# Pairing the two heads of a 128-partition block: score and value products of neighbourhood attention taken head beside head, the state product of linear attention in one operand

## The chip, the cores and the metric

The kernel runs on one core of a Trainium2 chip. The metric is the device time of one execution in microseconds (us); lower is better. A time is given as the median of several runs. A profiled execution gives the rows shown below: TensorE (PE, with its weight loads as PEld), VectorE (DVE), ScalarE (ACT), GpSimd (POOL), and the DMA queues.

## The reference, cut to what matters

Two layers are run over 640 tokens: 128 context tokens and 512 latent tokens, model width 1024. Each layer normalises its input, projects it, and feeds three groups in parallel; their outputs go through one output projection and are added to the input. An expert lookup (PEER) follows. Only two of the groups are touched here.

- **Linear attention**, 6 heads of 64, in both directions. For each chunk of tokens a 64x64 state per head and direction is read by the decayed queries:

```
inter = jnp.einsum('bhtk,bhkv->bhtv', qc * jnp.exp(cum), s)
...
return s_new, inter + intra
```

- **Neighbourhood attention**, 6 heads of 64. The latent tokens form a grid of 8 rows by 64 columns; a query sees the columns near its own (all 8 rows) and all 128 context keys, in one softmax. Context queries see the context keys only.

```
s_win = jnp.einsum('bhrqd,bhrkd->bhrqk', qg, kw).astype(jnp.float32) * scale + bias
s_win = jnp.where(col_mask[None, None, None], s_win, -1e30)
s_ctx = jnp.einsum('bhrqd,bhcd->bhrqc', qg, k_ctx).astype(jnp.float32) * scale
p = jax.nn.softmax(jnp.concatenate([s_win, s_ctx], axis=-1), axis=-1).astype(v.dtype)
```

## The kernel before, in words

Activations lie feature-major: features on the 128 partitions, tokens along the free axis. 128 partitions hold a pair of heads, head 0 of the pair on partitions 0 to 63 and head 1 on 64 to 127. There are three pairs (`fc` = 0, 1, 2) in each group and each layer (`l` = 0, 1), so a piece of work that is done once for a pair is done six times in all. Everything here is f32. An f32 matmul appears in the trace as two PE instructions (two passes), each with its own weight load; a transpose and an fp32r matmul appear as one.

`mix(l)` computes, in the order of the program, linear attention for three pairs (`pre`, line 286: the projections and decays; `gla`, line 316), one half of the convolution (`conv`, line 436), then neighbourhood attention for three pairs (`napre`, line 459: three projections and the transposed values; `na`, line 479), the other half of the convolution and the output projection. A projection (`projw`, line 218) is 48 fp32r matmuls at line 227 into two PSUM banks; its weights are split into a high and a low part by ACT (line 211) and DVE (line 212).

The order in which the instructions stand on an engine is fixed when the program is built and is not that of the text. A scheduler goes through the ready instructions in program order and puts later ones into the gaps. So in the trace the projections of pair `fc + 1` stand between the attention steps of pair `fc`, and in the last pair those of the convolution and of the output projection do. Buffers of one tag are handed out in program order: the PSUM tag "s" has four banks, and `ps_s` (scores), `pt` (transposes) and, in layer 0, the adaLN rows `ps_ada` and `ps_at` (lines 147 and 157) take turns in them.

**Neighbourhood attention** (`na`). For each head `hh` of the pair and each of five query tiles `qt` (one of context, four of latent tokens), one step is: scores against 1, 2 or 3 key tiles (line 493 or 500) and against the context keys (line 502), both with a contraction over the 64 partitions of that head; on DVE the bias is added and the maximum taken in one instruction (line 505); the maximum is negated (509); ACT takes the exponential with its sum (510); DVE inverts the sum and scales (511, 512); PE transposes the 1, 3 or 4 tiles of probabilities (516); ACT copies them out of PSUM (518); and PE multiplies them with the values (521), 64 output partitions wide, into the half of the bank `npo` that belongs to the head. Per head the five tiles have 1, 3, 4, 4 and 3 key tiles, 15 in all. Head 0 goes through all five tiles before head 1. In layer 0 a piece of the adaLN matmuls (`ada_steps`, line 152) is drawn after each tile of head 1. Those put four blocks of 32 output partitions into one bank.

**Linear attention** (`gla`). `qz[d]` holds the decayed queries of direction `d` twice: slot 0 has head 0 on partitions 0 to 63 and zeros below, slot 1 zeros and then head 1. Both slots are needed at line 355, where the two heads have to stay apart. The zeros are written once per layer (line 283). The states `sts[d]` are block-diagonal, with zeros off the diagonal (line 284). Line 413 multiplies each slot with the state: four matmuls for each of four latent chunks, two heads by two directions, all into one accumulation. Line 323 writes `qz` anew for the next pair. Line 333 multiplies keys and queries of each head, contraction over 64 partitions, into one bank for each head.

Of the kernel before, what the change touches and what calls it, by code (L numbers as in the profile page):

```python
# [10 lines left out]
F32 = mybir.dt.float32  # L11
# [12 lines left out]
TP, TS = 128, 512  # L24
# [9 lines left out]
NAK = [(0, 2), (0, 3), (1, 3), (2, 2)]  # L34
BOFF = {0: (0, 384), 1: (384, 512), 2: (384, 512), 3: (896, 384)}
BW = 1280
C_BADA, C_N1, C_N2, C_BAF, C_BAB, C_CW, C_CB, C_GN, C_FN = 0, 48, 56, 64, 67, 70, 76, 78, 81
NVEC = 89
CH_LR, CH_Q, CH_K, CH_V, CH_G, CH_CH, CH_CB, CH_CC, CH_QN, CH_KN, CH_VN = 0, 1, 4, 7, 10, 13, 15, 17, 19, 22, 25
# [26 lines left out]
class Trunk:  # L66
# [164 lines left out]
    def mix(self, l):  # L231
        tc, nc, I, O = self.tc, self.nc, self.I, self.O
        V, S, G, PE = self.V, self.S, self.G, self.PE
# [82 lines left out]
        def gla(fc, X):  # L316
# [20 lines left out]
            for lb in range(7):  # L337
# [38 lines left out]
                    nt.append(t2)  # L376
                tot = nt
            for d in range(2):
                kt = gp.tile([128, 5, 128], F32, name="kt", tag="kt")
                tokmajor(kS[d], kt)  # L380
                pk = pss.tile([128, 128], F32, name="pk", tag="s")
                PE.matmul(pk, kt[:, 0, :], vt[:, 0, :], start=True, stop=True)
                so = gp.tile([128, 64], F32, name="so", tag="so", bufs=2)
                for hh in range(2):
                    r = slice(64 * hh, 64 * hh + 64)
                    S.activation(so[r, :], pk[r, r], AF.Copy)
                nc.sync.dma_start(O["st"][l, d, fc], so)
                s = sts[d]
                order = range(4) if d == 0 else range(3, -1, -1)
                prev = None  # L390
                pk = pss.tile([128, 4, 128], F32, name="pk", tag="s")
                for c in order:
                    if prev is None:
                        for hh in range(2):
                            r = slice(64 * hh, 64 * hh + 64)
                            nc.sync.dma_start(s[r, c, r], I["st0"][l, d, fc, r, :])
                    else:
                        PE.matmul(pk[:, prev, :], kt[:, prev + 1, :], vt[:, prev + 1, :], start=True, stop=True)
                        for hh in range(2):
                            r = slice(64 * hh, 64 * hh + 64)  # L400
                            V.scalar_tensor_tensor(s[r, c, r], s[r, prev, r], tot[d][r, prev + 1:prev + 2],
                                                   pk[r, prev, r], op0=OP.mult, op1=OP.add)
                    prev = c
            for g, (c0, c1) in enumerate(CG):
                n = c1 - c0
                po = pss.tile([128, 4, 128], F32, name="po", tag="s")
                for c in range(n):
                    cs = slice((c + c0) * 128, (c + c0 + 1) * 128)
                    first = True
                    if g:  # L410
                        for d in range(2):
                            for hh in range(2):
                                PE.matmul(po[:, c, :], qz[d][:, hh, cs], sts[d][:, c, :], start=first, stop=False)
                                first = False
                    for hh in range(2):
                        r = slice(64 * hh, 64 * hh + 64)
                        PE.matmul(po[:, c, r], att[:, c0 + c, hh, :], vt[:, c0 + c, r], start=not g,
                                  stop=bool(hh) or not g)
                pv = po[:, :n, :].rearrange("p c (h v) -> p (c h) v", h=2)
                sq = gp.tile([128, 8, 64], F32, name="osq", tag="osq")  # L420
                S.activation(sq[:, :2 * n, :], pv, AF.Square)
                ms = gp.tile([128, 8], F32, name="oms", tag="oms", bufs=2)
                V.tensor_reduce(ms[:, :2 * n], sq[:, :2 * n, :], axis=AX.X, op=OP.add)
                S.activation(ms[:, :2 * n], ms[:, :2 * n], AF.Sqrt, bias=eps, scale=1.0 / 64)
                V.reciprocal(ms[:, :2 * n], ms[:, :2 * n])
                on = gp.tile([128, 4, 128], F32, name="on", tag="on")
                V.tensor_tensor(on[:, :n, :].rearrange("p c (h v) -> p (c h) v", h=2), pv,
                                ms[:, :2 * n][:, :, None].to_broadcast([128, 2 * n, 64]), op=OP.mult)
                pt = pss.tile([128, 4, 128], F32, name="pt", tag="s")
                for c in range(n):  # L430
                    PE.transpose(pt[:, c, :], on[:, c, :], ident)
                ts = slice(c0 * 128, c1 * 128)
                V.scalar_tensor_tensor(yT[:, fc, ts], pt[:, :n, :].rearrange("p c t -> p (c t)"),
                                       vec[:, l, C_GN + fc:C_GN + fc + 1], gs[:, ts], op0=OP.mult, op1=OP.mult)

        def conv(c):
            up = scr("up", 644)
# [41 lines left out]
        def na(fc, Y):  # L479
            q, k, vt = Y["q"], Y["k"], Y["vt"]  # L480
            po = [pss.tile([128, 4, 128], F32, name="npo", tag=f"o{i}", bufs=1) for i in range(2)]
            for hh in range(2):
                r = slice(64 * hh, 64 * hh + 64)
                bt = np_.tile([128, BW], F32, name="bt", tag="bt", bufs=2)
                nc.sync.dma_start(bt, I["bias"][l, 2 * fc + hh])
                for qt in range(5):
                    ps = pss.tile([128, 512], F32, name="ps_s", tag="s")
                    qs = slice(qt * 128, qt * 128 + 128)
                    s = np_.tile([128, 512], F32, name="ss", tag="ss", bufs=3)
                    mx = np_.tile([128, 4], F32, name="mx", tag="mx", bufs=4)  # L490
                    if qt == 0:
                        N = 128
                        PE.matmul(ps[:, :128], q[r, qs], k[r, :128], start=True, stop=True)
                        vs = [vt[:, 0, r]]
                        V.tensor_reduce(mx[:, 0:1], ps[:, :N], axis=AX.X, op=OP.max)
                        src = ps
                    else:
                        kt0, kn = NAK[qt - 1]
                        N = (kn + 1) * 128
                        PE.matmul(ps[:, :kn * 128], q[r, qs], k[r, (1 + kt0) * 128:(1 + kt0 + kn) * 128],  # L500
                                  start=True, stop=True)
                        PE.matmul(ps[:, kn * 128:N], q[r, qs], ck[r, fc, :], start=True, stop=True)
                        vs = [vt[:, 1 + kt0 + i, r] for i in range(kn)] + \
                             [cv[:, fc * 128 + 64 * hh:fc * 128 + 64 * hh + 64]]
                        V.tensor_tensor_reduce(out=s[:, :N], in0=ps[:, :N],
                                               in1=bt[:, BOFF[qt - 1][0]:BOFF[qt - 1][0] + N], scale=1.0,
                                               scalar=-3e38, op0=OP.add, op1=OP.max, accum_out=mx[:, 0:1])
                        src = s
                    V.tensor_scalar(mx[:, 1:2], mx[:, 0:1], -1.0, None, op0=OP.mult)
                    S.activation(s[:, :N], src[:, :N], AF.Exp, bias=mx[:, 1:2], accum_out=mx[:, 2:3])  # L510
                    V.reciprocal(mx[:, 3:4], mx[:, 2:3])
                    V.tensor_scalar(s[:, :N], s[:, :N], mx[:, 3:4], None, op0=OP.mult)
                    pt = pss.tile([128, 4, 128], F32, name="pt", tag="s")
                    nk = N // 128
                    for i in range(nk):
                        PE.transpose(pt[:, i, :], s[:, i * 128:(i + 1) * 128], ident)
                    pT = np_.tile([128, 4, 128], F32, name="pT", tag="pT", bufs=2)
                    S.activation(pT[:, :nk, :], pt[:, :nk, :], AF.Copy)
                    o = po[0][r, 0, :] if qt == 0 else po[1][r, qt - 1, :]
                    for i in range(nk):  # L520
                        PE.matmul(o, vs[i], pT[:, i, :], start=(i == 0), stop=(i == nk - 1))  # L521
                    if hh:
                        next(adas, None)
            S.activation(yT[:, 5 + fc, :TP], po[0][:, 0, :], AF.Copy)
            S.activation(yT[:, 5 + fc, TP:].rearrange("p (r ct c) -> p ct r c", r=8, ct=4),
                         po[1].rearrange("p ct (r c) -> p ct r c", r=8), AF.Copy)
# [480 lines left out]
```

## Time and profile before

| what | value |
|---|---|
| median of 3 runs | 4021.07 us (4016.36 to 4039.53) |
| profiled execution, own time | 4023.4 us |
| span of its trace | 4021.6 us |
| PE busy | 3681.0 us, 92% |
| DVE busy | 3260.8 us, 81% |
| ACT busy | 1635.8 us, 41% |
| POOL busy | 849.6 us, 21% |

The busy share of an engine is a mean over stages with different limits: the two `mix` stages lie at the start of the span and from about 2000 us on, the expert lookups behind each of them. PE's matmuls overlap, so what one costs is read from start to start, not from its duration: a row "x8" that starts at 149.63 and is followed by a row at 150.59 took 0.96 us for eight.

### The profile page before, as it was taken

How to read it: one execution, taken by the hardware profiler on the slowest of the kernel's cores; microseconds unless marked ns; L12 is line 12 of the kernel's file. 1: busy time of each engine (PE TensorE's matmuls, PEld its weight loads, DVE VectorE, ACT ScalarE, POOL GpSimd, SP SyncE). 2: the span in 40 equal slices, each digit the busy share in tenths (PEclk: the TensorE clock that was granted, in tenths of full speed). 3: DMA queues.
4: the chain of work that ended last, by engine and by line, in shares of the span. 5: the costliest groups of instructions: out<-in, count | busy, mean ns of one | idle time of the engine just before them, and what ended most of it. 6: DMA issues, size and time to landing. Idle time of an engine off the chain costs nothing.

```text
span 4021.6 us, 52975 instructions
## 1 busy us (share of the span) xinstructions
PE 3681.0 (92%) x19892; PEld 3167.7 (79%) x19892; DVE 3260.8 (81%) x6551; ACT 1635.8 (41%) x3125; POOL 849.6 (21%) x594
## 2 busy tenths in 40 slices
PE   7999987869999999999989999867799999999998
PEld 5897875557888888888869988745688888888886
DVE  3863369889999999999968533988899999999997
ACT  5423334863333333333354242378333333333332
POOL 0000010113333333333300000111233333333331
PEclk8999998989999999999989999878899999999998
DMA  5114233859999999999911121123899999999995
GB/s 181 33 63 138 71 116 107 250 194 375 361 379 369 388 378 385 382 384 380 352 49 34 63 66 53 33 83 110 296 379 374 386 372 380 384 380 385 371 386 194
DMA packets 263090, 1011.80 MB, mean 252 GB/s; under 512 B 21872, under 2 KB 110320, under 8 KB 164272
## 3 DMA queue, kind: packets, MB, share of 16 engines
q0 software_dynamic: 73728, 536.90, 34.7%
q1 hardware_dynamic: 171392, 425.43, 28.8%
q10 hardware_dynamic: 17712, 46.07, 2.9%
q8 instruction: 157, 2.57, 0.3%
q14 instruction: 101, 0.83, 0.1%
HBM read 960.49 MB, written 47.84 MB: 251 GB/s over the span
## 4 chain that ended last, share of the span: by engine, by line
PE 33%; issue 32%; POOL 11%; DVE 9%; ACT 8%; DMA 7%; POOLq 0%; ACTq 0%; DVEq 0%
PE ps_pj L227 13%; POOL uv L749 11%; DMA uv<-uv,gidx 6%; PE acc L874 4%; ACT qg L791 3%; PE ps_lv L355 2%; PE ps_g L794 2%; PE ps_ada L152 1%; ACT sg L799 1%; PE npo L521 1%; PE ps_ms L169 1%; PE ps_a L858 1%; PE ps_a L856 1%; PE ps_a L857 1%; PE ps_s L500 1%
## 5 line engine op out<-in xcount | busy, mean ns | idle before, releaser
L749 POOL DMA_INDIRECT uv<-uv,gidx x512 | 749.0, 1463 | 1531.6 <-DVE gacc L761 1374.1
L858 PE MATMUL ps_a<-hd,ulo 128*128 128x384 f32 x2048 | 693.2, 338 | 33.8 <-DVE ulo L836 33.8
L856 PE MATMUL ps_a<-hd,uhi 128*128 128x384 f32 x2048 | 690.8, 337 | 19.0 <-ACT uhi L835 19.0
L752 DVE SCALAR_TENSOR_TENSOR uv<-uv,ht 128x1024 f32<-128x1024 f32 x512 | 623.1, 1220 | 95.8 <-DMA uv<-uv,gidx 94.6
L857 PE MATMUL ps_a<-hd,uhi 128*128 128x384 f32 x2048 | 689.3, 337 | 0.0
L761 DVE SCALAR_TENSOR_TENSOR gacc<-uv,gw,gacc 128x1024 f32<-128x1024 f32 x508 | 652.3, 1284 | 14.8
L874 PE MATMUL acc<-vhi,whi 128*128 128x512 f32 x1536 | 506.2, 411 | 39.7 <-ACT whi L866 39.4
L874 PE MATMUL acc<-vhi,wlo 128*128 128x512 f32 x1536 | 484.8, 397 | 13.6 <-DVE wlo L867 13.4
L835 ACT ACTIVATE vhi<-raw 128x1024 fp32r<-128x1024 f32 x256 | 271.4, 1060 | 552.8 <-PE acc L874 536.5
L874 PE MATMUL acc<-vlo,whi 128*128 128x512 f32 x1536 | 479.3, 393 | 0.0
L858 PEld LDWEIGHTS ps_a<-hd,ulo 128*128 128x128 f32 x2048 | 386.3, 189 | 42.3 <-DVE ulo L836 39.5
L856 PEld LDWEIGHTS ps_a<-hd,uhi 128*128 128x128 f32 x2048 | 386.9, 189 | 29.7 <-ACT uhi L835 19.4
L857 PEld LDWEIGHTS ps_a<-hd,uhi 128*128 128x128 f32 x2048 | 386.9, 189 | 10.1
L874 PEld LDWEIGHTS acc<-vhi,whi 128*128 128x128 f32 x1536 | 271.2, 189 | 133.3 <-ACT whi L866 86.9
L874 PEld LDWEIGHTS acc<-vhi,wlo 128*128 128x128 f32 x1536 | 282.1, 188 | 92.1 <-DVE wlo L867 33.1
L874 PEld LDWEIGHTS acc<-vlo,whi 128*128 128x128 f32 x1536 | 290.3, 189 | 66.4
L794 PE MATMUL ps_g<-ohp,qg 128*128 128x128 f32 x1536 | 268.8, 316 | 76.3 <-ACT qg L791 75.7
L794 PEld LDWEIGHTS ps_g<-ohp,qg 128*128 128x128 f32 x1536 | 216.4, 205 | 142.5 <-ACT qg L791 116.9
L836 DVE TENSOR_TENSOR ulo<-raw,uhi 128x1024 fp32r<-128x1024 f32 x256 | 312.4, 1220 | 14.8 <-DMA gsp<-sg 13.5
L836 DVE TENSOR_TENSOR vlo<-raw,vhi 128x1024 fp32r<-128x1024 f32 x256 | 312.0, 1219 | 7.3 <-ACT vhi L835 7.1
L754 ACT ACTIVATE gw<-dots 128x2 f32<-128x2 f32 x256 | 52.0, 203 | 621.4 <-DVE uv L752 621.3
L227 PE MATMUL ps_pj<-hhi,whi 128*128 128x320 f32 x896 | 286.0, 322 | 17.7 <-ACT hhi L203 10.2
(240 smaller groups left out, 6104.3 us busy)
## 6 DMA issues: line engine op xcount, KB each, us to landing
raw<-dn SPq DMA_DIRECT2D x256, 1024.0 KB
wada<-w_ada SPq DMA_DIRECT2D x48, 1024.0 KB
gsp<-sg SPq DMA_DIRECT2D x48, 896.0 KB
gres<-gsp ACTq DMA_DIRECT2D x112, 384.0 KB
wraw<-w_in SPq DMA_DIRECT2D x56, 512.0 KB
wraw<-w_out SPq DMA_DIRECT2D x16, 512.0 KB
wraw<-wq SPq DMA_DIRECT2D x16, 512.0 KB
uv<-uv,gidx POOLq DMA_INDIRECT x512, 6.8
```

The source lines that it names most:

```text
L227: self.PE.matmul(ps[j][:, :n], w[:, k, :], x[:, k, :], start=(k == 0 and i == 0), stop=(k == 7 and i == 2))
L749: G.indirect_dma_start(out=b, out_offset=None, in_=I["uv"], in_offset=bass.IndirectOffsetOnAxis(ap=gidx[t][:, s:s + 1], axis=0))
L752: V.scalar_tensor_tensor(b[:, :D], b[:, :D], 1.0, ht[t], op0=OP.mult, op1=OP.mult, accum_out=dots[:, s:s + 1])
L761: V.scalar_tensor_tensor(acc_, b[:, D:], w[:, s:s + 1], acc_, op0=OP.mult, op1=OP.add)
L791: S.activation(qg[:, t, :], ohq[:, :, t4 + t], AF.Copy, scale=gT[:, t0 + t4 + t:t0 + t4 + t + 1])
L794: PE.matmul(ps[:, t, :], qg[:, t, :], ohp[:, t4 + t, :], start=True, stop=True)
L835: S.activation(hi, raw, AF.Copy)
L836: V.tensor_tensor(lo, raw, hi.bitcast(F32), op=OP.subtract)
L856: PE.matmul(ps, uhi[:, ks], hd[0][:, k, :], start=(k == 0), stop=False)
L857: PE.matmul(ps, uhi[:, ks], hd[1][:, k, :], start=False, stop=False)
L858: PE.matmul(ps, ulo[:, ks], hd[0][:, k, :], start=False, stop=(k == 7))
L874: PE.matmul(acc[:, t, j, :], a[:, ts], x[:, j * 512:(j + 1) * 512], start=(b == 0 and i == 0), stop=(b == 127 and i == len(parts) - 1))
```

## The change

In `na` the loop over heads becomes the inner one. Both biases of the pair are loaded at the start (four buffers in place of two). For each query tile the scores of both heads are issued next to each other, into two banks; the softmax, the transposes and the copies are done for one head and then for the other; and the value products alternate between the heads, key tile by key tile. `ss` and `pT` have four buffers in place of three and two. In `gla`, before the state products, GpSimd copies the latent part of head 1's half of slot 1 into slot 0, so that slot 0 holds both heads; line 413 then needs one matmul per direction and chunk. After the outputs of the first and second pair GpSimd writes zeros back.

```diff
+HR = (slice(0, 64), slice(64, 128))
...
             for d in range(2):
+                G.tensor_copy(qz[d][64:, 0, TP:], qz[d][64:, 1, TP:])
+            for d in range(2):
                 kt = gp.tile([128, 5, 128], F32, name="kt", tag="kt")
...
-                    first = True
                     if g:
                         for d in range(2):
-                            for hh in range(2):
-                                PE.matmul(po[:, c, :], qz[d][:, hh, cs], sts[d][:, c, :], start=first, stop=False)
-                                first = False
+                            PE.matmul(po[:, c, :], qz[d][:, 0, cs], sts[d][:, c, :], start=not d, stop=False)
...
+            if fc < 2:
+                for d in range(2):
+                    G.memset(qz[d][64:, 0, TP:], 0.0)
...
+            bts = []
             for hh in range(2):
-                r = slice(64 * hh, 64 * hh + 64)
-                bt = np_.tile([128, BW], F32, name="bt", tag="bt", bufs=2)
+                bt = np_.tile([128, BW], F32, name="bt", tag="bt", bufs=4)
                 nc.sync.dma_start(bt, I["bias"][l, 2 * fc + hh])
-                for qt in range(5):
-                    ps = pss.tile([128, 512], F32, name="ps_s", tag="s")
-                    qs = slice(qt * 128, qt * 128 + 128)
-                    s = np_.tile([128, 512], F32, name="ss", tag="ss", bufs=3)
+                bts.append(bt)
+            for qt in range(5):
+                qs = slice(qt * 128, qt * 128 + 128)
+                kt0, kn = (-1, 1) if qt == 0 else NAK[qt - 1]
+                N = 128 if qt == 0 else (kn + 1) * 128
+                nk = N // 128
+                pss2 = [pss.tile([128, 512], F32, name="ps_s", tag="s") for hh in range(2)]
+                for hh, r in enumerate(HR):
+                    PE.matmul(pss2[hh][:, :kn * 128], q[r, qs], k[r, (1 + kt0) * 128:(1 + kt0 + kn) * 128],
+                              start=True, stop=True)
+                if qt:
+                    for hh, r in enumerate(HR):
+                        PE.matmul(pss2[hh][:, kn * 128:N], q[r, qs], ck[r, fc, :], start=True, stop=True)
+                pTs = []
+                for hh, ps in enumerate(pss2):
+                    s = np_.tile([128, 512], F32, name="ss", tag="ss", bufs=4)
...
-                        PE.matmul(ps[:, :128], q[r, qs], k[r, :128], start=True, stop=True)
...
-                        PE.matmul(ps[:, :kn * 128], q[r, qs], k[r, (1 + kt0) * 128:(1 + kt0 + kn) * 128],
-                                  start=True, stop=True)
-                        PE.matmul(ps[:, kn * 128:N], q[r, qs], ck[r, fc, :], start=True, stop=True)
...
-                    pT = np_.tile([128, 4, 128], F32, name="pT", tag="pT", bufs=2)
+                    pT = np_.tile([128, 4, 128], F32, name="pT", tag="pT", bufs=4)
                     S.activation(pT[:, :nk, :], pt[:, :nk, :], AF.Copy)
-                    o = po[0][r, 0, :] if qt == 0 else po[1][r, qt - 1, :]
-                    for i in range(nk):
-                        PE.matmul(o, vs[i], pT[:, i, :], start=(i == 0), stop=(i == nk - 1))
-                    if hh:
-                        next(adas, None)
+                    pTs.append(pT)
+                for i in range(nk):
+                    for hh, r in enumerate(HR):
+                        o = po[0][r, 0, :] if qt == 0 else po[1][r, qt - 1, :]
+                        v = vt[:, 1 + kt0 + i, r] if i < kn else cv[:, fc * 128 + 64 * hh:fc * 128 + 64 * hh + 64]
+                        PE.matmul(o, v, pTs[hh][:, i, :], start=(i == 0), stop=(i == nk - 1))
+                next(adas, None)
```

## Rows read from the trace of the kernel before

**Rows 1.** Busy time by stretch: linear attention, neighbourhood attention (layer 0), neighbourhood attention (layer 1).
```profile
core 0: us, PE busy (x) PEld busy (x) DVE busy (x) ACT busy (x) POOL busy (x), PEclk, DMA share, GB/s
95.00:283.00 188.00, 182.54 (x1351) 170.90 (x1351) 143.23 (x295) 67.90 (x111) 0.00 (x0) 1.00 0.13 39
283.00:466.00 183.00, 178.91 (x1102) 139.27 (x1102) 64.33 (x185) 68.43 (x157) 0.00 (x0) 0.99 0.36 118
...
2281.00:2446.00 165.00, 160.71 (x981) 134.60 (x979) 63.59 (x180) 66.39 (x153) 0.00 (x0) 0.99 0.20 66
```

**Rows 2.** What PE waited for from 2285 to 2446 us (all rows).
```profile
PE ps_pj L227 <- ACT yhi L554: 2.3, 1, 2.3
PE ps_pj L227 <- ACT nq L467: 1.4, 1, 1.4
```

**Rows 3.** Timeline of PE in neighbourhood attention, layer 0.
```profile
304.48 0.48 PE L493 MATMUL ps_s<-nk,nq 64*128 64x128 f32 x2
304.89 0.41 PE L227 MATMUL ps_pj<-hhi,whi 128*128 128x320 f32 x1
...
318.84 0.91 PE L500 MATMUL ps_s<-nk,nq 64*128 64x384 f32 x2
...
319.90 0.87 PE L521 MATMUL npo<-pT,nv 128*64 128x128 f32 x6
...
320.92 0.41 PE L227 MATMUL ps_pj<-hhi,wlo 128*128 128x320 f32 x1
321.17 0.31 PE L227 MATMUL ps_pj<-hhi,whi 128*128 128x320 f32 x1
321.31 0.31 PE L227 MATMUL ps_pj<-hlo,whi 128*128 128x320 f32 x1
...
323.16 0.70 PE L500 MATMUL ps_s<-nk,nq 64*128 64x256 f32 x2
...
324.01 0.41 PE L227 MATMUL ps_pj<-hlo,whi 128*128 128x320 f32 x1
...
328.12 0.65 PE L521 MATMUL npo<-pT,nv 128*64 128x128 f32 x4
...
328.92 0.41 PE L227 MATMUL ps_pj<-hlo,whi 128*128 128x320 f32 x1
```

**Rows 4.** Timeline of PE in linear attention, layer 0: state product, key-query product, level products.
```profile
149.63 1.13 PE L413 MATMUL po<-st,qz 128*128 128x128 f32 x8
150.59 0.56 PE L417 MATMUL po<-vt,att 128*128 128x64 f32 x4
...
165.27 1.78 PE L333 MATMUL ps_d<-q,kS 64*128 64x128 f32 x20
166.98 0.72 PE L355 MATMUL ps_lv<-qz,kS 128*128 128x128 f32 x4
```

**Rows 5.** Timeline of PE around an adaLN piece in layer 0.
```profile
329.67 1.05 PE L152 MATMUL ps_ada<-wada,sc 128*32 128x512 f32 x2
330.64 0.43 PE L521 MATMUL npo<-pT,nv 128*64 128x128 f32 x2
331.00 1.06 PE L152 MATMUL ps_ada<-wada,sc 128*32 128x512 f32 x6
331.99 0.70 PE L500 MATMUL ps_s<-nk,nq 64*128 64x256 f32 x2
```

**Rows 6.** Timeline of DVE: the last level's write of `qz` in the first pair.
```profile
139.61 0.83 DVE L369 TENSOR_TENSOR qz<-qz,tot 128x640 f32<-128x640 f32 x1
```

**Rows 7.** Groups of POOL over the whole span (busy, mean ns of one).
```profile
L787 POOL TENSOR_TENSOR qg<-ohq,gT 128x512 f32<-128x512 bf16 x48 | 59.1, 1232 | 427.5 <-PE ps_g L794 372.4 <-DVE ohq L783 31.9 <-issue 11.7
...
L283 POOL MEMSET qz<- 64x640 f32 x8 | 5.0, 627 | 14.6 <-DVE gacc L761 14.1 <-POOLq L998 0.3
```

**Rows 8.** Timeline, one softmax step in layer 1: its bias-and-maximum, the next scores.
```profile
2425.45 0.69 DVE L505 CUSTOM_DVE_ANT_0 ss<-ps_s,bt 128x512 f32<-128x512 f32 x1 [0.95 <-PE ps_s L502]
...
2428.61 0.59 PE L500 MATMUL ps_s<-nk,nq 64*128 64x384 f32 x1
```

More of the change, by code (lines that the diff above doesn't have):

```diff
@@ L481, in na @@
             po = [pss.tile([128, 4, 128], F32, name="npo", tag=f"o{i}", bufs=1) for i in range(2)]
+            bts = []
             for hh in range(2):
-                r = slice(64 * hh, 64 * hh + 64)
-                bt = np_.tile([128, BW], F32, name="bt", tag="bt", bufs=2)
+                bt = np_.tile([128, BW], F32, name="bt", tag="bt", bufs=4)
                 nc.sync.dma_start(bt, I["bias"][l, 2 * fc + hh])
-                for qt in range(5):
-                    ps = pss.tile([128, 512], F32, name="ps_s", tag="s")
-                    qs = slice(qt * 128, qt * 128 + 128)
-                    s = np_.tile([128, 512], F32, name="ss", tag="ss", bufs=3)
+                bts.append(bt)
[14 more added lines that the diff above has]
+                    s = np_.tile([128, 512], F32, name="ss", tag="ss", bufs=4)
                     mx = np_.tile([128, 4], F32, name="mx", tag="mx", bufs=4)
                     if qt == 0:
-                        N = 128
-                        PE.matmul(ps[:, :128], q[r, qs], k[r, :128], start=True, stop=True)
-                        vs = [vt[:, 0, r]]
                         V.tensor_reduce(mx[:, 0:1], ps[:, :N], axis=AX.X, op=OP.max)
@@ L497, in na @@
                     else:
-                        kt0, kn = NAK[qt - 1]
-                        N = (kn + 1) * 128
-                        PE.matmul(ps[:, :kn * 128], q[r, qs], k[r, (1 + kt0) * 128:(1 + kt0 + kn) * 128],
-                                  start=True, stop=True)
-                        PE.matmul(ps[:, kn * 128:N], q[r, qs], ck[r, fc, :], start=True, stop=True)
-                        vs = [vt[:, 1 + kt0 + i, r] for i in range(kn)] + \
-                             [cv[:, fc * 128 + 64 * hh:fc * 128 + 64 * hh + 64]]
                         V.tensor_tensor_reduce(out=s[:, :N], in0=ps[:, :N],
-                                               in1=bt[:, BOFF[qt - 1][0]:BOFF[qt - 1][0] + N], scale=1.0,
+                                               in1=bts[hh][:, BOFF[qt - 1][0]:BOFF[qt - 1][0] + N], scale=1.0,
                                                scalar=-3e38, op0=OP.add, op1=OP.max, accum_out=mx[:, 0:1])
@@ L513, in na @@
                     pt = pss.tile([128, 4, 128], F32, name="pt", tag="s")
-                    nk = N // 128
                     for i in range(nk):
                         PE.transpose(pt[:, i, :], s[:, i * 128:(i + 1) * 128], ident)
-                    pT = np_.tile([128, 4, 128], F32, name="pT", tag="pT", bufs=2)
+                    pT = np_.tile([128, 4, 128], F32, name="pT", tag="pT", bufs=4)
                     S.activation(pT[:, :nk, :], pt[:, :nk, :], AF.Copy)
-                    o = po[0][r, 0, :] if qt == 0 else po[1][r, qt - 1, :]
-                    for i in range(nk):
-                        PE.matmul(o, vs[i], pT[:, i, :], start=(i == 0), stop=(i == nk - 1))
-                    if hh:
-                        next(adas, None)
+                    pTs.append(pT)
[5 more added lines that the diff above has]
+                next(adas, None)
             S.activation(yT[:, 5 + fc, :TP], po[0][:, 0, :], AF.Copy)
```

## The prediction

> **What bounds the kernel now.** I read three views, all of the two attention stretches, since the change touches nothing else. First the busy time by stretch [rows 1]: in linear attention PE is busy 182.5 of 188 us, in neighbourhood attention 178.9 of 183 (layer 0) and 160.7 of 165 (layer 1), at a granted clock of 0.99 to 1.00. No other engine is above 143 of 188 in the first, or 69 of 183 in the second. A busy PE can hide idle time, so second the waits of PE [rows 2]: in the 161 us from 2285 to 2446 it waited twice, 3.7 us in all. Third PE's own timeline [rows 3], read from start to start: between attention blocks stand projections of the next pair (line 227), with no gap. So PE's issue is the limit here; what leaves PE's stream is time, as long as other work is ready to close up, and the projections are that work.
>
> **Parts, from rows.** In neighbourhood attention a head's score block with three key tiles starts at 318.84 (its context keys, line 502, right behind) and the next work at 319.90: 1.06 us. With two key tiles 323.16 to 324.01, 0.85; the context tile 304.48 to 304.89, 0.41. A value block of four key tiles takes 319.90 to 320.92, 1.02; of three, 328.12 to 328.92, 0.80 [rows 3]; of one, 330.64 to 331.00, 0.36 [rows 5]. A head has one context tile, two of the small and two of the large latent tiles: scores 0.41 + 2 x 0.85 + 2 x 1.06 = 4.23 us, values 0.36 + 2 x 0.80 + 2 x 1.02 = 4.00 us, together 8.23 us.
>
> **Does a pair take the time of one?** Two places of the old kernel bear on it. Column halves (the value products): one adaLN block of 32 output partitions takes two passes, 329.67 to 330.64, 0.97 us; three blocks side by side take six passes from 331.00 to 331.99, 0.99 us [rows 5]. So blocks on different output partitions, with weights and moving data of their own and in one bank, run at once. Row halves (the scores): line 333 sends twenty passes of 128 columns with the heads on different partitions. They take 165.27 to 166.98, 1.71 us [rows 4], 86 ns each, where eight passes of the value block took 1.02, 128 ns each. Ten pairs at half price would be about 10 x 0.107 = 1.07 (0.107 is 128 columns at the 0.32 of a 384-column pass, below) plus 0.2 for the change of shape in and out, 1.27; 0.44 us went astray over its three groups of chunks, 0.15 a group. So row halves run at once too, with some loss.
>
> The 0.32 and the 0.2: the three-key-tile block has two passes of 384 and two of 128 columns, 1024 columns in 1.06 us, the two-tile block 768 in 0.85. The difference, 0.21 us for 256 columns, is 0.32 for 384 and 0.107 for 128, and leaves about 0.2 a block that doesn't depend on columns: the change of tile shape. The same cost sits outside of a block: the first projection after one holds the stream for 0.25 us (320.92 to 321.17), the second for 0.14 (321.17 to 321.31) [rows 3].
>
> **The sum.**
> 1. Scores and values: six pairs, each with one head's 8.23 us less: 49.4 us. This has the blocks' own shape changes in it.
> 2. Sixty blocks fewer stand between projections and transposes. The 0.11 us of the first projection behind each [rows 3] and a like step into the block lie outside of it, 0.2 in all, but blocks that follow each other share them: I take 0.12, so 7 us.
> 3. State product: eight passes took 149.63 to 150.59, 0.96 us [rows 4]; four go. Four chunks by six pairs by 0.48: 11.5 us.
> 4. Loss of pairing, 0.15 a group as at line 333, over the 60 paired blocks: 9 us back. The last pair of a layer has no next pair to fill with; its step is longer for two heads (below), about 1 us a layer: 2 us back.
>
> 49.4 + 7 + 11.5 - 9 - 2 = 57 us. Against the profiled execution's own span of 4021.6 us that gives 3964.6; its own time was 4023.4, and the median of the runs 4021.07, so I give 3964 for the median.
>
> **What is added, and what covers it.** GpSimd gets twelve copies of 64 x 512 and eight memsets of that size. It has no such copy in the trace: the memset of 64 x 640 at 0.627 us is a floor, the two-operand 128 x 512 at 1.232 a ceiling [rows 7]; I take 0.9, between them as it has one operand to read. In these stretches GpSimd has no work at all [rows 1]. The copies can start when the last level has written `qz`, 139.61 + 0.83 [rows 6], and the first state product is at 149.63 [rows 4]: 9 us for two copies of at most 1.23. The memsets follow the last state product (four blocks of some 1.35 after 149.63, so about 155); the first reader of the zeros is line 355 at 166.98 [rows 4]: 12 us for two of at most 0.63. VectorE's line 323 writes other parts of the same tile; were it held behind the memsets, that is 1.3 us, with line 355 still 8 us off. So I cost both at nothing. If all cover were gone it would be 12 x 1.23 + 8 x 0.63 = 20 us. The twelve bias loads stay twelve on the SP queue; with four buffers they are issued earlier, in stretches with a DMA share of 0.13 to 0.36 [rows 1]: nothing, and below a microsecond either way. DVE and ACT keep their instructions one for one.
>
> [...] The trace's value block issues eight passes in 1.02 us, each with its own weight load, and three adaLN blocks load six sets of weights within the 0.99 us of their matmuls [rows 3, 5]: loads on one set of rows hide behind matmuls in flight. [...]
>
> **Rivals.**
> - *The softmax chain takes over.* One head's step now goes from its bias instruction at 2425.45 to the next scores at 2428.61, 3.16 us, and with its score block 4.2 [rows 8, 3]. For two heads in step the second waits for the first one's DVE work, 0.69 and the small instructions behind it; I estimate 5.1 to 6 us, and up to 7 where weight splits stand in between. PE's work after the change is some (165 - 28) / 15 = 9 us a pair step in layer 1, fillers included, and more in layer 0. So the chain should hide. If it took 10 in layer 1, that layer would be at 150 and the gain there 15 us and not 28: 3977 to 3985. Chance 0.10.
> - *No overlap.* Tiles of the two heads wait for each other. Then only shape changes go: 60 x 0.2 + 7, plus the state product's 11.5, less 9 + 2: 20 us, 4001. Against it stand rows 4 and 5. Chance 0.06, half of it within 0.5%.
> [...]
> - *Slower: PSUM banks.* A pair step takes two score banks and two transpose banks, all four of tag "s", which adaLN in layer 0 shares. If the scores of the next tile can be issued only when both heads' probabilities have been copied out, and PE's order puts them ahead of the projections, PE stands still. Layer 1's stretch now has 165 / 15 = 11 us a pair step; from 11.4 on (the state product's 11.5 over 30 steps more) the kernel is slower than now. At 12.5 us: 30 x 1.5 less the state product's 11.5, 34 us over, 4055. Against it: the score banks are read by the bias instruction alone and free before the transposes. Chance 0.04.
> - *The gain is given back*, by the order in which the scheduler puts what follows: within 0.5%. Chance 0.04.
>
> **Chances and range.** My forecast has 0.72. About 0.5% (20 us, below 4001) is what a measurement of this kernel can tell from no change. Faster: 0.72 + 0.10 + 0.03 + 0.04 = 0.89; within: 0.03 + 0.04, 0.07; slower 0.04. The range goes down to all gains with no loss, 68 us, and the waits of [rows 2] gone in both layers, 7 us: 3946. It goes up over the chain and the open loads to 3995. It leaves out no overlap, the given-back gain and the slower case, some 0.14, and a little below.
>
> **What would show it.** In the changed kernel's PE timeline, rows of line 502's successor with four passes in about the time of two; a value block of sixteen passes in about 1.1 us; a state block of four passes in about 0.5 us; the neighbourhood stretches shorter by 25 us each and the linear ones by about 6; PE's waits there still a few us. It would be wrong if pair blocks take 1.7 us and more (no overlap), if PE's waits on ACT's copies or on DVE in those stretches come to over 10 us (the chain, or the banks), or if the stretches shrink and the lookup behind them grows.

## The result, and the profile after

The changed kernel takes **3975.4 us** (median of 5 runs, 3966.73 to 4007.9) beside 4023.06 us for the kernel before in the same comparison (5 runs, 4016.36 to 4039.53). The ratio is 0.9891, 95% interval 0.987 to 0.9912: 44 us less by the ratio (35 to 52), 48 us by the medians. Forecast were 3964 us, in a range from 3946 to 3995, and faster. The profiled execution took 3966.73 us, 56.7 us less than the profiled one of before.

The page of the changed kernel, its busy times:

```profile
PE 3633.4 (92%) x19796; PEld 3133.0 (79%) x19796; DVE 3255.5 (82%) x6551; ACT 1633.4 (41%) x3125; POOL 856.9 (22%) x614
```

PE is 48 us less busy. GpSimd, with its new copies and memsets, is 7 us more, DVE and ACT 5 and 2 us less. Where it went is read by stretch. I take neighbourhood attention together with the output projection behind it, so that work which the scheduler moves from one to the other stays inside: from the first query evacuation to the last residual add. Busy time by stretch, before, layers 0 and 1:

```profile
core 0: us, PE busy (x) PEld busy (x) DVE busy (x) ACT busy (x) POOL busy (x), PEclk, DMA share, GB/s
287.70:530.60 242.90, 239.07 (x1477) 196.22 (x1477) 81.46 (x214) 79.61 (x171) 0.00 (x0) 0.99 0.28 93
2284.50:2507.50 223.00, 217.90 (x1333) 187.99 (x1333) 79.57 (x207) 76.45 (x165) 0.00 (x0) 0.99 0.17 54
```

The same two stretches in the changed kernel:

```profile
284.00:508.00 224.00, 219.76 (x1477) 181.98 (x1477) 77.92 (x214) 77.61 (x172) 0.00 (x0) 0.99 0.32 102
2260.00:2464.00 204.00, 199.82 (x1333) 173.81 (x1333) 76.09 (x207) 74.69 (x165) 0.00 (x0) 1.00 0.18 60
```

PE has the same 1477 and 1333 instructions and is busy 19 and 18 us less: the same passes, more of them at once. What PE still waited for in layer 1's neighbourhood stretch, from 2250 to 2420 us (all rows; the rest of the stretch, to 2464 us, adds none):

```profile
PE ps_pj L228 <- ACT yhi L560: 1.6, 1, 1.6
PE ps_pj L228 <- ACT nq L470: 1.4, 1, 1.4
PE ps_pj L228 <- DVE ylo L561: 0.8, 1, 0.8
```

The first two are the waits of [rows 2] again, and the third is a small one beside them: 3.8 us in place of 3.7. None is on the softmax chain or on a bank. So PE's stream is still the limit.

**The paired blocks.** PE's timeline in layer 0, a whole value block and a whole score block (three key tiles and context; line 497 was 500, 501 was 502, 528 was 521):

```profile
322.46 0.88 PE L528 MATMUL npo<-pT,nv 128*64 128x128 f32 x12
323.16 0.39 PE L528 MATMUL npo<-pT,cv 128*64 128x128 f32 x4
323.48 1.06 PE L153 MATMUL ps_ada<-wada,sc 128*32 128x512 f32 x6
324.47 0.92 PE L497 MATMUL ps_s<-nk,nq 64*128 64x384 f32 x4
325.22 0.39 PE L501 MATMUL ps_s<-ck,nq 64*128 64x128 f32 x4
325.54 1.07 PE L153 MATMUL ps_ada<-wada,sc 128*32 128x512 f32 x8
```

Read from start to start, sixteen value passes take 322.46 to 323.48, 1.02 us, where eight took 1.02 [rows 3]. Eight score passes take 324.47 to 325.54, 1.07, where four took 1.06. A pair costs what one head cost, with nothing lost. The same kind of step in layer 1 looks different:

```profile
2293.70 0.91 PE L497 MATMUL ps_s<-nk,nq 64*128 64x384 f32 x2
2294.54 0.88 PE L528 MATMUL npo<-pT,nv 128*64 128x128 f32 x12
2295.24 0.39 PE L528 MATMUL npo<-pT,cv 128*64 128x128 f32 x4
2295.56 0.59 PE L497 MATMUL ps_s<-nk,nq 64*128 64x384 f32 x1
2295.57 0.49 PE L501 MATMUL ps_s<-ck,nq 64*128 64x128 f32 x2
2295.99 0.48 PE L497 MATMUL ps_s<-nk,nq 64*128 64x384 f32 x1
2296.31 0.38 PE L501 MATMUL ps_s<-ck,nq 64*128 64x128 f32 x2
...
2296.62 0.41 PE L228 MATMUL ps_pj<-hhi,wlo 128*128 128x320 f32 x1
```

Head 0's two local score passes run alone (2293.70 to 2294.54, 0.84 us). Then come sixteen value passes of the tile before. The other six score passes follow from 2295.56 to 2296.62, 1.06 us: as long as the whole pair needs. This block cost 0.84 + 1.06 = 1.90 us in place of 1.07. My explanation is that the scheduler goes through ready work in program order: value products stand earlier in the program than the next tile's scores, so when they became ready after head 0's first scores, they went in between. The experiment with the scores ahead of the values tests it. I call this a **split pair**.

**Linear attention**, PE's timeline around the state product (line 414 was 413):

```profile
151.58 0.68 PE L414 MATMUL po<-st,qz 128*128 128x128 f32 x4
152.10 0.56 PE L417 MATMUL po<-vt,att 128*128 128x64 f32 x4
152.49 0.66 PE L414 MATMUL po<-st,qz 128*128 128x128 f32 x4
152.99 0.56 PE L417 MATMUL po<-vt,att 128*128 128x64 f32 x4
...
166.53 0.72 PE L356 MATMUL ps_lv<-qz,kS 128*128 128x128 f32 x4
```

Four passes take 0.52 and 0.50 us, where eight took 0.96 [rows 4]. GpSimd's new work, in its timeline and its groups:

```profile
140.12 0.61 POOL L380 COPY qz<-qz 64x512 f32<-64x512 f32 x1 [135.75 <-DVE qz L370]
141.97 0.72 POOL L380 COPY qz<-qz 64x512 f32<-64x512 f32 x1 [1.24 <-PE pt L275]
154.84 0.98 POOL L437 MEMSET qz<- 64x512 f32 x2 [12.15 <-PE po L414]
...
L380 POOL COPY qz<-qz 64x512 f32<-64x512 f32 x12 | 10.7, 900 | 441.3 <-DVE qz L370 319.7 <-issue 116.6 <-PE pt L275 5.0
```

The copies end at 142.69, 9 us ahead of the state product at 151.58; the memsets end at 155.82, 11 us ahead of the next reader, line 356 at 166.53.

The table sums up all kernels. Columns: length of the linear stretch (first key-query product to last output product) and of the neighbourhood stretch as above, for layers 0 / 1; and, out of the neighbourhood stretch, PE's time in scores and in values, each pass taken from its own start to the next one's, and the number of times that consecutive passes change tile shape.

| kernel | linear | neighbourhood | scores | values | shape changes |
|---|---|---|---|---|---|
| before | 181.6 / 181.6 | 242.9 / 223.0 | 27.0 / 27.3 | 24.7 / 24.9 | 128 / 110 |
| **after** | 176.7 / 177.2 | 223.5 / 203.7 | 17.8 / 22.1 | 15.3 / 15.4 | 88 / 75 |
| neighbourhood part alone | 181.6 / 181.6 | 223.5 / 205.2 | 17.8 / 22.1 | 15.3 / 15.4 | 88 / 75 |
| state product alone | 176.7 / 176.9 | 242.9 / 224.4 | 27.0 / 28.1 | 24.1 / 24.9 | 128 / 110 |
| scores apart | 176.9 / 177.3 | 231.5 / 216.9 | 25.8 / 26.1 | 17.4 / 19.5 | 120 / 105 |
| **scores ahead of values** | 176.7 / 176.7 | 210.0 / 193.5 | 12.8 / 12.8 | 12.8 / 13.2 | 63 / 54 |
| scores a step ahead | 176.7 / 176.7 | 224.4 / 200.3 | 14.8 / 18.6 | 15.7 / 15.7 | 99 / 72 |
| copies three times | 178.6 / 179.0 | 222.0 / 205.3 | 17.8 / 22.1 | 15.3 / 15.4 | 88 / 75 |
| values head by head | 176.9 / 176.9 | 223.6 / 206.2 | 15.1 / 19.8 | 19.0 / 18.0 | 72 / 59 |
| values apart | 176.7 / 177.2 | 223.3 / 207.8 | 17.8 / 18.2 | 23.3 / 22.7 | 77 / 67 |

Before to after, the linear stretches give 4.9 + 4.4 = 9.3 us and the neighbourhood stretches 19.4 + 19.3 = 38.7: **48 us**, the difference of the medians. Of the other 8.7 between the two profiled executions 7.8 lie in the lookups, which the change doesn't touch (from the end of a neighbourhood stretch to the next linear stretch, and in layer 1 to the last product of the lookup): 1567.6 and 1478.7 us before, 1570.5 and 1468.0 after. Over all the profiles above they scatter from 1567 to 1580 and from 1467 to 1484.

### The profile page after: what moved, and what is told of

It is laid out like the page before. It is cut to its first block, busy times and chain, and to the rows that moved or that the text cites. A ratio compares the mean times of both kernels' runs of the same rounds, so it can differ in the third digit from the quotient of the medians.

```text
span 3964.9 us, 52896 instructions
## 1 busy us (share of the span) xinstructions
PE 3633.4 (92%) x19796; PEld 3133.0 (79%) x19796; DVE 3255.5 (82%) x6551; ACT 1633.4 (41%) x3125; POOL 856.9 (22%) x614
## 4 chain that ended last, share of the span: by engine, by line
PE 33%; issue 31%; POOL 10%; DVE 10%; ACT 8%; DMA 7%; POOLq 0%; ACTq 0%; DVEq 0%
PE ps_pj L228 13%; POOL uv L755 10%; DMA uv<-uv,gidx 7%; PE acc L880 4%; ACT qg L797 3%; PE ps_lv L356 2%; PE ps_g L800 2%; ACT sg L805 1%; PE ps_ada L153 1%; PE ps_a L864 1%; PE ps_a L862 1%; PE ps_a L863 1%; PE ps_ms L170 1%; PE ps_s L497 1%; PE npo L528 1%
## 5 line engine op out<-in xcount | busy, mean ns | idle before, releaser
L864 PEld LDWEIGHTS ps_a<-hd,ulo 128*128 128x128 f32 x2048 | 386.3, 189 | 32.2 <-DVE ulo L842 29.5
```

Of the source, the lines that this page charges most:

```text
L864: PE.matmul(ps, ulo[:, ks], hd[0][:, k, :], start=False, stop=(k == 7))
```

## The experiments

### Each part alone

First, the neighbourhood part without the state product's (no copies, the old four state matmuls):

```diff
-                G.tensor_copy(qz[d][64:, 0, TP:], qz[d][64:, 1, TP:])
...
-                            PE.matmul(po[:, c, :], qz[d][:, 0, cs], sts[d][:, c, :], start=not d, stop=False)
+                            for hh in range(2):
+                                PE.matmul(po[:, c, :], qz[d][:, hh, cs], sts[d][:, c, :], start=first, stop=False)
+                                first = False
...
-                    G.memset(qz[d][64:, 0, TP:], 0.0)
```

> Only the neighbourhood part of the change; the state product is as before (eight passes a chunk, no copies, no zeros written back). Theory (what leaves TensorE's stream is the gain, part by part): the linear-attention stretches go back to their old 181.6 us each (first key-query product to last output product), the neighbourhood stretches (first query evacuation to the last residual add of the output projection) stay at the changed kernel's 223.5 and 203.7 us; about 39 us less than the kernel before, some 3984 us. Rival (the two parts share a gain, for instance by the order of the work): the neighbourhood stretches differ by more than 3 us from the changed kernel's.

Measured: 3987.61 us (3985.72 to 3999.31) beside 4022.08 (15 runs of before, shared with the next three); ratio 0.9916, 0.9891 to 0.9941. Its neighbourhood stretches are those of the full change within 1.5 us, its linear ones those of before.

Second, the other way round: the kernel before with the copies, one matmul a direction and chunk, and the memsets.

```diff
+                G.tensor_copy(qz[d][64:, 0, TP:], qz[d][64:, 1, TP:])
...
-                            for hh in range(2):
-                                PE.matmul(po[:, c, :], qz[d][:, hh, cs], sts[d][:, c, :], start=first, stop=False)
+                            PE.matmul(po[:, c, :], qz[d][:, 0, cs], sts[d][:, c, :], start=not d, stop=False)
...
+                    G.memset(qz[d][64:, 0, TP:], 0.0)
```

> Only the linear-attention part: GpSimd copies, one matmul per direction and chunk, zeros written back; neighbourhood attention as before. Theory: linear-attention stretches of 176.7 and 177.1 us as in the changed kernel, neighbourhood stretches at the old 242.9 and 223.0; 9 to 10 us less in all, within 0.5% of the kernel before. Rival (copies or zeros are waited for): the stretches shrink by less than 3 us or not at all.

Measured: 4018.9 us (4015.42 to 4028.32); ratio 0.9991, 0.998 to 1.0003. The timing can't tell this part from nothing; the trace can: the linear stretches are 4.9 and 4.7 us shorter, and the neighbourhood stretches lie within 1.4 us of before. The two ratios multiply to 0.9907, beside 0.9891 for both: the parts add up, and the neighbourhood part has four fifths of the gain.

### Is it the standing side by side?

Each head's scores go back into its own part of the softmax loop, so that transposes and softmax work stand between the two heads' scores. Everything else is the changed kernel.

```diff
-                pss2 = [pss.tile([128, 512], F32, name="ps_s", tag="s") for hh in range(2)]
+                pTs = []
                 for hh, r in enumerate(HR):
+                    ps = pss.tile([128, 512], F32, name="ps_s", tag="s")
...
-                for hh, ps in enumerate(pss2):
```

> The changed kernel, but the scores of the second head are issued in its own part of the softmax loop, so that the score blocks of a pair no longer stand next to each other; the values stay paired. Theory (row halves run at once only when they stand next to each other): the score lines cost what they cost before, 26 to 27 us a layer from start to start against 17.8 (layer 0) and 22.1 (layer 1) in the changed kernel, so the neighbourhood stretches grow by 9 to 14 us in layer 0 and 5 to 10 in layer 1: some 3992 us. Rival (the gain is only fewer changes of tile shape, or comes from the values alone): the score lines stay within 3 us a layer of the changed kernel's.

Measured: 4001.33 us (3998.57 to 4009.06); ratio 0.994, 0.9918 to 0.9961. Scores are back at 25.8 / 26.1 us, near the 27.0 / 27.3 of before, and 26 us of the gain are gone with them (4001.33 - 3975.4). Values rise too, 15.3 to 17.4 and 15.4 to 19.5: in PE's order the first two passes of every value block now stand apart from the rest, most of them with projections behind them. The same passes run on the same halves of the array; only their order on PE differs. So it is adjacency that makes the gain.

### Scores of the next tile ahead of the values

If split pairs are what is missing, the scores of the next tile must not be overtaken. They become a function, called for tile `qt + 1` right ahead of the value products of tile `qt`:

```diff
-            for qt in range(5):
+            def scores(qt):
...
+                return pss2
+
+            pss2 = scores(0)
+            for qt in range(5):
...
+                nxt = scores(qt + 1) if qt < 4 else None
                 for i in range(nk):
                     for hh, r in enumerate(HR):
...
+                pss2 = nxt
```

> The changed kernel, with the scores of the next query tile written in the program ahead of this tile's value products, so that TensorE's order has every score block whole (eight passes) and followed directly by the value block. Theory (the change fell short of its sum because value products that become ready split the score pairs): score lines at about 14 us a layer (from 17.8 and 22.1), value lines at 12.5 to 14 (from 15.3), fewer changes of shape; neighbourhood stretches of about 215 and 191 us (from 223.5 and 203.7), some 20 us less than the changed kernel, 3955 us. Rival (the softmax chain or the four score banks bind): the passes get cheaper but TensorE's waits in these stretches grow by as much, and the stretches shrink by less than 4 us each.

Measured: **3951.05 us** (3948.02 to 3965.44, 5 runs); ratio 0.9834, 0.981 to 0.9858. That is 71 us less than before and 24 us less than the change: a version that beats both. Its busy time by stretch, and PE's timeline of one step in layer 0:

```profile
283.00:493.00 210.00, 205.65 (x1477) 177.59 (x1477) 77.77 (x215) 78.53 (x171) 0.00 (x0) 1.00 0.33 109
2246.00:2439.00 193.00, 188.67 (x1333) 169.53 (x1333) 77.01 (x207) 74.16 (x164) 0.00 (x0) 1.00 0.20 64
...
315.26 0.92 PE L497 MATMUL ps_s<-nk,nq 64*128 64x384 f32 x4
316.01 0.39 PE L501 MATMUL ps_s<-ck,nq 64*128 64x128 f32 x4
316.32 0.88 PE L536 MATMUL npo<-pT,nv 128*64 128x128 f32 x12
317.03 0.39 PE L536 MATMUL npo<-pT,cv 128*64 128x128 f32 x4
317.35 1.92 PE L153 MATMUL ps_ada<-wada,sc 128*32 128x512 f32 x16
```

Eight score passes (1.06 us), sixteen value passes (1.03), nothing in between. All twelve later tiles of each layer have their eight score passes together, and scores fall to 12.8 us in both layers.

### Scores a whole step ahead

The same function, called ahead of the softmax of tile `qt` and not of its value products, so that PE would never wait for a softmax:

```diff
                 nk = N // 128
+                nxt = scores(qt + 1) if qt < 4 else None
                 pTs = []
```

> The kernel with the scores ahead of the values, but a whole step earlier: the scores of the next tile are written ahead of this tile's softmax, so that four score banks are in flight and the transposes come behind them. Theory (TensorE's stream is the limit and the softmax chain is covered already): an earlier start buys nothing; TensorE's order now has the first value product of most tiles apart from the others, so the value lines cost 1 to 3 us a layer more than in that kernel (12.8 and 13.2), stretches of 210 to 214 and 194 to 198 us. Rival (the softmax chain still costs something): stretches shorter by 3 us or more each, below 207 and 190.

Measured: 3973.56 us (3965.59 to 3980.02) beside 4024.38 (7 runs of before, shared with the next three); ratio 0.988, 0.9863 to 0.9896. It missed: 224.4 / 200.3 us of neighbourhood stretch, where the theory had 210 to 214 and 194 to 198, and no better in time than the change. PE's timeline shows one reason:

```profile
2287.15 0.70 PE L497 MATMUL ps_s<-nk,nq 64*128 64x256 f32 x2
2287.78 0.97 PE L536 MATMUL npo<-pT,nv 128*64 128x128 f32 x12
...
2288.89 0.48 PE L497 MATMUL ps_s<-nk,nq 64*128 64x256 f32 x1
```

The pair is split again, in 2 tiles of layer 0 and 9 of layer 1. As the scores of tile `qt + 1` were issued early, those of `qt + 2` come into PE's order while the values of `qt` wait, and these stand earlier in the program. That is not all of it: scores still cost less than in the change (14.8 / 18.6 for 17.8 / 22.1). In layer 0 the adaLN matmuls (line 153) take back what the scores give: read from start to start they cost 22.6 us, where they cost 17.8 in the change and 13.6 with the scores directly ahead. Earlier is not better; directly ahead of the values is.

### The GpSimd copies, three times over

```diff
-            for d in range(2):
+            for d in [0, 1] * 3:
                 G.tensor_copy(qz[d][64:, 0, TP:], qz[d][64:, 1, TP:])
```

> The changed kernel with every GpSimd copy of head 1's half made three times over. Theory (the copies lie wholly beside other work, with about 9 us between the last write of the queries and the first state product): linear-attention stretches stay at 176.7 and 177.2 us, within 0.7. Rival (they are on the path, or slow VectorE down): the stretches grow by three pairs times the added copies, 3 us or more a layer.

Measured: 3968.0 us (one run). The linear stretches grow by 1.9 and 1.8 us over the changed kernel's, between what the two theories said. GpSimd's timeline, and DVE's beside it:

```profile
139.77 6.20 POOL L380 COPY qz<-qz 64x512 f32<-64x512 f32 x6 [135.40 <-DVE qz L370]
...
140.65 1.23 DVE L370 TENSOR_TENSOR qz<-qz,tot 128x640 f32<-128x640 f32 x1
141.80 0.90 DVE L372 TENSOR_TENSOR kS<-kS,tot 128x320 f32<-128x320 f32 x1
142.62 1.63 DVE L213 TENSOR_TENSOR wlo<-wraw,whi 128x1024 fp32r<-128x1024 f32 x1
...
PE pk L401 <- DVE st L404: 1.5, 3, 0.7
```

The copies end at 145.97, still inside their cover; the state product starts at 152.06 in place of 151.58, which is 0.84 us later from the start of its stretch (102.35 and 102.71). DVE's first two instructions in the fence take longer than in the changed kernel. In that one the first of them lies between the two copies (140.12 to 140.73 and 141.97 to 142.69), the second reaches 0.25 us into the second copy, and the third begins beside it:

```profile
141.00 0.81 DVE L370 TENSOR_TENSOR qz<-qz,tot 128x640 f32<-128x640 f32 x1
141.74 0.48 DVE L372 TENSOR_TENSOR kS<-kS,tot 128x320 f32<-128x320 f32 x1
142.14 1.63 DVE L213 TENSOR_TENSOR wlo<-wraw,whi 128x1024 fp32r<-128x1024 f32 x1
```

0.81 became 1.23, 0.48 became 0.90: 0.42 us each. With three times the copies DVE's state update (line 404) is late, and PE waits 1.5 us for it (the last line of the first fence), a wait that the changed kernel doesn't have. So the copies of the change are hidden, but not as idle GpSimd time alone would say: they also cost DVE time (line 213 took 1.63 us, where it took 1.23 in the kernel before), and PE's waits show none on it.

### Values head by head

The value products of head 0, then those of head 1, in place of alternating:

```diff
-                for i in range(nk):
-                    for hh, r in enumerate(HR):
+                for hh, r in enumerate(HR):
+                    for i in range(nk):
```

> The changed kernel with the value products of a tile written head after head and not alternating; they stay neighbours in TensorE's order. Theory (TensorE itself runs passes of different tiles at once, whatever their order within the queue, as line 333 shows for row halves): a block of sixteen value passes still takes about 1.0 us, value lines within 1.5 us of the changed kernel's 15.3 a layer. Rival (strictly in order: the second head's passes start behind the first head's last one): a block of sixteen takes 1.7 to 1.9 us, value lines 22 us or more.

Measured: 3976.61 us (one run), values 19.0 / 18.0 us: neither theory. One block of sixteen passes in PE's timeline, layer 0:

```profile
321.76 0.93 PE L528 MATMUL npo<-pT,nv 128*64 128x128 f32 x8
322.46 0.27 PE L528 MATMUL npo<-pT,cv 128*64 128x128 f32 x1
322.52 0.27 PE L528 MATMUL npo<-pT,nv 128*64 128x128 f32 x1
322.57 0.27 PE L528 MATMUL npo<-pT,cv 128*64 128x128 f32 x1
322.63 0.49 PE L528 MATMUL npo<-pT,nv 128*64 128x128 f32 x3
322.96 0.38 PE L528 MATMUL npo<-pT,cv 128*64 128x128 f32 x2
323.27 0.63 PE L153 MATMUL ps_ada<-wada,sc 128*32 128x512 f32 x3
```

The block takes 321.76 to 323.27, 1.51 us: between 1.02 alternating and the 1.7 to 1.9 that were expected of one head after the other. Each head has six passes on `nv` and then two on `cv`. Eight `nv` passes start ahead of the first `cv`, so two of them are head 1's, started before head 0's last two, although they stand behind them in the program. It is not the scheduler's doing: in PE's order as it was built all of head 0's products of this block stand ahead of head 1's. So in this block PE ran passes of the other half beside ones that stand ahead of them, but the overlap was partial, 1.51 us. Of the two orders it is the alternating one that gave the full overlap, 1.02 us. The one run took as long as the change, since fewer pairs were split here: scores cost 5.0 us less in both layers together (15.1 / 19.8) and values 6.3 more.

### Values apart, with the scores ahead

The version with scores ahead, with `scores(qt + 1)` moved between the two heads' value products:

```diff
+                r = HR[0]
                 for i in range(nk):
...
+                nxt = scores(qt + 1) if qt < 4 else None
+                r = HR[1]
+                for i in range(nk):
```

> The kernel with the scores ahead of the values, with the next tile's scores put between the value products of the two heads, so that in 12 of 15 tiles the two value blocks don't touch. Scores stay paired. Theory (column halves run at once only when neighbours): value lines grow from 13 to 22 to 24 us a layer, with two changes of shape more in these tiles, stretches of 220 to 224 and 203 to 208 us, about 22 us more than 3951. Rival (the value products' gain came from fewer changes of shape): value lines stay below 17.

Measured: 3981.43 us (3977.55 to 3987.9); ratio 0.9897, 0.988 to 0.9913; 30 us over the version with scores ahead. Values are 23.3 / 22.7 us, near the 24.7 / 24.9 of before, so here column halves too took the time of one only side by side. Scores rose as well, to 17.8 / 18.2: here it is head 0's value products that split the score pairs.

**The price of a split pair.** Counting in PE's order the tiles (of twelve a layer with eight score passes) whose scores are cut by value products, mostly into two and six, gives nearly the same price in six stretches with different counts; 12.8 us is the stretch with none:

| stretch | split pairs | scores, us | over 12.8, per split |
|---|---|---|---|
| scores ahead, either layer | 0 | 12.8 | |
| values head by head, layer 0 | 3 | 15.1 | 0.77 |
| after, layer 0 | 7 | 17.8 | 0.71 |
| values apart, layer 0 | 7 | 17.8 | 0.71 |
| values apart, layer 1 | 7 | 18.2 | 0.77 |
| values head by head, layer 1 | 10 | 19.8 | 0.70 |
| after, layer 1 | 12 | 22.1 | 0.78 |

The kernel with the scores a step ahead doesn't fit as well, with 1.0 us for each of 2 splits (14.8 us) and 0.64 for each of 9 (18.6 us): there transposes and not values follow most score blocks, and some blocks of two tiles stand together.

## Why the prediction was right, point by point

**The bound** held: PE's stream was the limit and stayed it. Kernels that only reorder PE's work moved the time by about what their stretches say: 21 us longer and 26 slower with the scores apart, 24 shorter and 24 faster with the scores ahead. In layer 0 the last value product comes 34 us earlier (431.3 in place of 465.7) and the projections left over follow it; the stretch still ends 23.0 us earlier, 3.6 of it from the linear one and its start.

**"Does a pair take the time of one?"** Yes, for both kinds of halves: 1.07 for 1.06, 1.02 for 1.02. The no-overlap rival falls. No run shows the open weight loads for which the range goes up to 3995 and 0.04 of the chances is set aside: in their place the trace of the changed kernel has sixteen value passes, all on the same 128 rows and each with a load of its own (sixteen loads from 322.46 on), in 1.02 us. In the block taken head by head two passes started ahead of two that stand before them in PE's order (eight `nv` passes start ahead of the first `cv`, at 322.46).

**Terms 1 and 2, scores, values and shape changes, 56.4 us.** These are sizes without loss, so the version with scores ahead is their test: 32.9 + 29.5 = 62.4 us of neighbourhood stretch less. Scores give 14.2 + 14.5 = 28.7 (predicted 25.4), values 11.9 + 11.7 = 23.6 (24.0). The rest is 10: about 6 are in transposes (4.1) and projections (2.3), for which 7 were forecast, and 4.2 are in layer 0's adaLN matmuls, which no term had. With the scores ahead their passes stand together (sixteen from 317.35 in its timeline), and they cost 13.6 us in place of 17.8. So the terms were 6 us too small.

**Term 4, "loss of pairing, 0.15 a group", 9 us back, is the one that was mis-sized**, and its reason was wrong. I took the loss from line 333 as something each pair loses. Whole pairs lost nothing (1.07 for 1.06 us, 1.02 for 1.02); the changed kernel lost 62.4 - 38.7 = 23.7 us by its order: 5.0 + 9.3 in the 19 split pairs, 2.5 + 2.2 in value blocks cut up, 4.2 in the adaLN matmuls of layer 0, and 0.5 elsewhere. The prediction had the order of PE fixed by a scheduler, and did not ask whether it would keep the two heads together. Line 333 writes one head's passes and then the other's, as in the experiment that takes the values head by head; that its 0.44 us come from there was not tested. 9 + 2 us had been set aside for it, 12.7 too few. That the forecast came out near is in part luck: terms 1 and 2, 6 too small the other way, made good half of it.

**Term 3, the state product, 11.5 us.** Four passes cost 0.51 and not 0.48, as the first pass behind another line's cost more (0.18 us, from 151.58 to 151.76, where the three behind it took 0.34 together, to 152.10), so 24 x 0.45 = 10.8 us; the stretches gave 9.3 (4.9 and 4.4 us, where about 6 each were forecast). PE's waits in them are no longer than before. The last 1.5 us lie in PE's own passes: start to start those of the state update (`pk`, lines 382 and 398) cost 0.55 us a layer more, also in the kernel with the state product alone, and in layer 1 the level products and decays together 0.5 more. Why was not tested.

**What was costed at nothing** shows in no wait of PE. The copy's price, 0.9 us, was its mean, 900 ns, but that is a mean of copies from 0.61 to 1.85; the memset took 0.522 against 0.627 for a larger one. That copies and DVE's instructions would take longer beside each other (line 213 1.63 us for 1.23, a copy 1.85 for 0.61) was not thought of.

**The softmax chain and the PSUM banks**: no wait of PE on either appeared; both rivals fall. **The gain given back**: the lookups differ by +3 and -11 us, inside their scatter.

The sum, 57 us, met 48. Terms 1 to 3 gave 72 where no score pair was split (62.4 + 9.8, in the version with scores ahead, whose median is 71 us under before).

## What to carry to other kernels

In these runs two matmuls on different halves of the array took the time of one (1.07 us for 1.06, 1.02 for 1.02) only where they stood side by side, alternating, in the engine's order; after such a change look in the timeline for rows of the expected count, and count the blocks that were cut. Where a scheduler goes by program order, write the paired block directly ahead of the work that would otherwise get into it: here that was worth half as much again as the change itself, 24 us beside 48. When an idle engine takes over work, look also at what its neighbours' instructions cost meanwhile: here DVE's weight split took 1.63 us for 1.23.

## What was not expected of the hardware

Three two-operand instructions of DVE took 0.4 us longer beside GpSimd's copies: lines 370 and 372 went from 0.81 to 1.23 and from 0.48 to 0.90 in the first pair with the copies made three times, and line 213's weight split took 1.63 us in the changed kernel too, in the first two pairs of each layer, where the same instruction in the kernel before (line 212) took 1.23 with GpSimd idle. Not every one did: line 324, two operands on 64 partitions, took 0.82 us at 144.67 beside the threefold copies and 0.82 at 144.19 in the changed kernel with GpSimd idle. In the third pair it is the copy that took longer, 1.85 us in place of 0.61, and DVE's line 370 beside it kept its 0.82. From the timelines of DVE (before, then after) and of GpSimd (after):

```profile
140.75 1.23 DVE L212 TENSOR_TENSOR wlo<-wraw,whi 128x1024 fp32r<-128x1024 f32 x1
...
263.66 0.82 DVE L370 TENSOR_TENSOR qz<-qz,tot 128x640 f32<-128x640 f32 x1
...
263.50 1.85 POOL L380 COPY qz<-qz 64x512 f32<-64x512 f32 x1 [45.58 <-DVE qz L370]
```

What decides which instruction takes longer was not tested.

A value block whose halves come one after the other, eight passes each, still overlapped in part: 1.51 us, between 1.02 alternating and the 1.7 to 1.9 expected without overlap.
